# Giving the two operations that split a half block of weights a place ahead of all others in the scheduler

## The chip, the cores and the metric

The kernel runs on one core of one Trainium2 chip. The metric is the device time of one execution in microseconds (us); lower is better. Engines are called PE (TensorE, matrix products; PEld is its weight loading), DVE (VectorE), ACT (ScalarE), POOL (GpSimd) and SP (SyncE, which issues the DMAs). Each takes its instructions in one fixed order.

## The reference

Two residual blocks follow each other on x, 512 positions by 2048 channels, float32. What is computed, cut to the steps that cost time:

```
# first block
h = rms_norm(x) * (1 + scale) + shift;  p = h @ w_in
u = layer_norm(conv31(cv * sigmoid(cg)));  y_conv = (silu(u) * silu(cz)) @ w_conv_out
y_attn = (rms_norm(differential attention, 8 heads) * silu(az)) @ w_attn_out
x = x + gate * rms_norm((sigmoid(m1) * y_conv + sigmoid(m2) * y_attn) @ w_o)
# second block, on x (512 positions, "lat") and a context (256 positions, "ctx")
u = h @ w_in2                                  # h: 512 x 2048, w_in2: 2048 x 8,608
gated delta rule, 8 heads, both directions:    # conv5, l2norm, then by chunks of 64
    T = inverse(I + L);  v_new = T v - T k state;  o = q state + attn v_new
    state = state * decay + k^T v_new
RWKV-7 scan, 16 heads, both directions, by chunks in the kernel
x = rms_norm(x + gate * concat(delta rule, RWKV) @ w_out)
```

## The kernel before

A product with a weight matrix is called dense here. `mblock` makes 128 output columns in one accumulator (`pd`, two buffers) out of 16 blocks of 128 rows, in two half blocks of eight. `products` does a half block: one DMA brings 512 KB into `wraw` (three buffers), the split makes two reduced float32 parts of it, `whi` (a cast on ACT, line 105) and `wlo` (the difference, on DVE, line 106; during the first products of the context every second one is on POOL), each with two buffers, and 24 matmuls of line 157 follow: whi with the high part of the activations, whi with their low part, wlo with the high part, eight times. A half block can be cast when its `wraw` has landed and the matmuls of the half block before the last have let go of its `whi`.

The order on each engine is made by a list scheduler ahead of the run: among the instructions that its own model of time finds ready it takes the one with the lowest priority number, and the number grows with the order in which the program is written. `tc.cur_priority -= FIRST` (a million) puts what is issued until it is set back ahead of all else. In `products` that holds for the matmuls except every twelfth (`K.burst`; every sixth in the later parts), so that dense matmuls come in groups that nothing interrupts and between groups PE can turn to something else. In the same way `before` in the RWKV part adds 800 (`LATER`) to everything that the dense products written there issue.

The parts of the run that are spoken of: the products of the context with the delta rule's inputs (about 420 to 640 us of the trace), the delta rule on x (`mixers_gdn`, 2240 to 2950 us) and the RWKV part on x (`mixers_rwkv`, to 3830 us). In the delta rule each of eight heads is a sequence of three stretches, and the dense blocks of the next head (q, k, v, z, two half blocks each) are worked in between:

- preparation: Gram products (line 632), masks on DVE (`gd_kkd` and others), the first part of a triangular inverse on DVE (`iv_u8`, `iv_sh`, lines 368 to 383);
- the inverse on PE (lines 396 to 432, 692 to 717), with copies on ACT and DVE between;
- the chain over four steps (line 123 in `Visit.mm`): a product with `gd_uu` gives on DVE `gd_vn` (line 755), a product with `gd_ktl` gives the state `S` (line 775), a product with `S` gives `gd_R` (line 747), and so on. Each step waits for the one before.

The RWKV part has a similar chain: the products into `pc` and, on DVE, `rg_H` (lines 1060 and 1077).

Of the kernel before, what the change touches and what calls it, by code (L numbers as in the profile page):

```python
# [103 lines left out]
def split(K, hi, lo, src, eng=None):  # L104
    K.nc.scalar.copy(hi, src)  # L105
    (eng or K.nc.vector).tensor_tensor(lo, src, hi.bitcast(F32), op=ALU.subtract)  # L106


FIRST = 1000000
# [22 lines left out]
def mblock(K, wap, act, T, k0=0, k1=16, half=8):  # L132

    ps = K.pd.tile([128, 512], F32, name="pd")
    for ka in range(k0, k1, half):
        products(K, ps, wap, act[ka - k0:], T, ka, min(half, k1 - ka), k0, k1)
        K.fill()
    return ps[:, :T]


def products(K, ps, wap, act, T, ka, w, k0, k1):


    nc, tc = K.nc, K.tc
    raw = K.wp.tile([128, 8, 128], F32, name="wraw")
    hi = K.wp.tile([128, 8, 128], F32R, name="whi", bufs=2)
    lo = K.wp.tile([128, 8, 128], F32R, name="wlo", bufs=2)
    nc.sync.dma_start(raw[:, :w], wap[:, ka:ka + w, :])
    K.n_split += 1
    split(K, hi[:, :w], lo[:, :w], raw[:, :w], nc.gpsimd if K.on_pool and K.n_split % K.on_pool == 0 else nc.vector)  # L150
    for k in range(w):
        ah, al = act[k]
        for j, (a, b) in enumerate(((hi, ah), (hi, al), (lo, ah))):
            n = 3 * (ka - k0 + k) + j
            ahead = FIRST if n % K.burst else 0
            tc.cur_priority -= ahead
            nc.tensor.matmul(ps[:, :T], lhsT=a[:, k], rhs=b, start=(n == 0), stop=(n == 3 * (k1 - k0) - 1))  # L157
            tc.cur_priority += ahead
# [199 lines left out]
def inv64(K, pool, upool, nm, ds, px, tmp):  # L358
# [30 lines left out]
    for lev in range(2):  # L389
        yp, zp = products()  # L390
        ys = pool.tile([128, n, 32], F32, name="iv_y")
        for m in range(n):
            for r in range(4):
                q = slice(32 * r, 32 * r + 32)
                o = 32 * (r % 2)
                nc.tensor.matmul(yp[q, m], lhsT=nm[q, m, o:o + 32], rhs=t32[q, m], start=True, stop=True,
                                 tile_position=(32 * r, 32 * r))
        nc.scalar.copy(ys, yp)
        for m in range(n):
            for r in range(4):  # L400
                q = slice(32 * r, 32 * r + 32)
                nc.tensor.matmul(zp[q, m], lhsT=ys[q, m], rhs=u32[q, m], start=True, stop=True,  # L402
                                 tile_position=(32 * r, 32 * r))
        for d, m0, w in orders:
            nc.vector.copy_predicated(u32[:, m0:m0 + w], K.cp[d, lev].unsqueeze(1).to_broadcast([128, w, 32]),  # L405
                                      zp[:, m0:m0 + w])
        nc.vector.transpose(t32.rearrange("p n e -> p (n e)"), u32.rearrange("p n e -> p (n e)"))

    u64 = upool.tile([128, n, 64], F32, name="iv_u64")
    for b in range(2):  # L410
        nc.vector.tensor_scalar(u64[:, :, 32 * b:32 * b + 32], u32, c["m64"][:, b:b + 1], None, op0=ALU.mult)
    yp, zp = products()
    ys = pool.tile([128, n, 32], F32, name="iv_y")

# [1432 lines left out]
```

## Time and profile before

| | |
|---|---|
| three runs | 3966.07, 3958.37, 3956.31 us (median 3958.37) |
| the profiled execution | 3948.75 us, of which the span from first to last instruction is 3947.0 us |
| PE busy | 3672.7 us, 93% of the span |
| DVE / ACT / POOL busy | 70% / 34% / 13% |
| mean granted clock of PE | 0.962 of full speed |

A busy share counts the time in which an instruction of the engine is under way; matmuls overlap, so one may last 0.4 us while they follow each other every 0.23 us. In a view of waits the numbers are the total wait in us, the number of times and the longest. In a timeline a row gives the start, the time until the end of the group, engine, line, operation, output<-input and count, and in brackets how long the engine sat idle before it and what ended that. In a table of windows each engine has its busy us and number of instructions; the three numbers at the end are PE's granted clock (1.00 is 2.4 GHz, 0.50 is 1.2 GHz), the busy share of the DMA engines, and GB/s.

### The profile page before, as it was taken

The page shows a single profiled execution, that of the slowest core. Times are in us where ns is not written, and L with a number is a line of the kernel's source. Part 1 is how long each engine was busy: PE and PEld are TensorE (multiplying, and loading weights), DVE is VectorE, ACT ScalarE, POOL GpSimd, SP SyncE. Part 2 cuts the span into 40 slices and gives each one's busy share as a digit, 9 for nine tenths or more (in the row PEclk, how much of TensorE's full clock was granted, in tenths as well). Part 3 has the DMA queues.
Part 4 walks back from the last instruction along what each step waited for, and adds up shares of the span by engine and source line. Part 5 has one row for each costly group of instructions (what it writes and reads, how often), then busy time and mean ns, then how long its engine had stood idle before and what let it go on. Part 6 is the DMA issues. An engine that isn't in the chain of part 4 may idle for free. (4 is left out here: it accounts for less than half of the span.)

```text
span 3947.0 us, 81802 instructions
## 1 busy us (share of the span) xinstructions
PE 3672.7 (93%) x33066; PEld 2837.3 (72%) x33066; DVE 2748.4 (70%) x7146; ACT 1359.4 (34%) x2713; POOL 505.4 (13%) x595
## 2 busy tenths in 40 slices
PE   8899878999999999999998889989999999998997
PEld 4577678876777777777886577777877777766676
DVE  3366798788778778553524877776767778877866
ACT  3322333323334344332322432322323444444333
POOL 0100231003101001000311201100001111111102
PEclk9999899999999999999999999999999999999998
DMA  8766445423433333425523222222223122212235
GB/s 321 269 226 216 161 133 173 140 102 127 136 118 107 118 111 126 130 81 179 204 93 129 101 88 68 67 69 75 86 79 110 65 68 81 68 67 83 91 129 203
DMA packets 206491, 492.95 MB, mean 125 GB/s; under 512 B 40096, under 2 KB 71328, under 8 KB 202016
## 3 DMA queue, kind: packets, MB, share of 16 engines
q1 hardware_dynamic: 206112, 487.72, 36.4%
q8 instruction: 260, 4.26, 0.4%
q14 instruction: 119, 0.97, 0.1%
HBM read 434.54 MB, written 53.09 MB: 124 GB/s over the span
## 5 line engine op out<-in xcount | busy, mean ns | idle before, releaser
L157 PE MATMUL pd<-big,whi 128*128 128x512 f32 x5280 | 1759.5, 411 | 8.0 <-ACT big L352 8.0
L157 PEld LDWEIGHTS pd<-big,whi 128*128 128x128 f32 x5280 | 964.4, 192 | 251.4 <-issue 20.8
L157 PE MATMUL pd<-big,wlo 128*128 128x512 f32 x2768 | 1104.2, 399 | 24.3 <-DVE wlo L106 23.6
L105 ACT CAST whi<-wraw 128x1024 fp32r<-128x1024 f32 (+2 forms) x498 | 502.9, 1010 | 1159.5 <-PE pd L157 1074.7
L106 DVE TENSOR_TENSOR wlo<-wraw,whi 128x1024 fp32r<-128x1024 f32 (+2 forms) x478 | 572.9, 1199 | 318.4 <-ACT whi L105 311.2
L157 PEld LDWEIGHTS pd<-big,wlo 128*128 128x128 f32 x2768 | 530.0, 191 | 147.1 <-DVE wlo L106 28.2
L157 PE MATMUL pd<-hc,whi 128*128 128x256 f32 x1152 | 227.0, 297 | 11.5 <-ACT hc L352 5.5
L157 PE MATMUL pd<-hc,wlo 128*128 128x256 f32 x576 | 171.7, 298 | 33.0 <-DVE wlo L106 23.9
L157 PEld LDWEIGHTS pd<-hc,whi 128*128 128x128 f32 x1152 | 188.3, 199 | 15.3 <-ACT hc L352 5.6
L157 PE MATMUL pd<-ext,whi 128*128 128x512 f32 x512 | 184.6, 401 | 3.8 <-DVE ext L106 3.8
L1160 DVE SCALAR_TENSOR_TENSOR cv_y<-cv_up,vec,cv_y 128x512 f32<-128x512 f32 x240 | 180.9, 754 | 4.2
L157 PE MATMUL pd<-fa,whi 128*128 128x512 f32 x448 | 149.9, 414 | 0.9 <-ACT fa L105 0.8
L157 PEld LDWEIGHTS pd<-hc,wlo 128*128 128x128 f32 x576 | 114.8, 199 | 40.0 <-DVE wlo L106 28.0
L944 POOL TENSOR_TENSOR rg_bk<-rg_th,rg_L 64x512 f32<-64x512 f32 x48 | 69.1, 1439 | 400.5 <-ACT rg_L L923 274.0
L1055 ACT ACTIVATE rg_zw<-rg_H,rg_wc 64x64 f32<-64x64 f32 x320 | 102.8, 342 | 43.4 <-DVE rg_H L1077 39.2
L157 PEld LDWEIGHTS pd<-ext,whi 128*128 128x128 f32 x512 | 97.3, 190 | 27.9 <-DVE ext L106 4.7
L1077 DVE SCALAR_TENSOR_TENSOR rg_H<-pc,rg_wc,rg_zw 64x64 f32<-64x64 f32 x320 | 90.4, 282 | 33.7 <-PE pc L123 24.0
L567 DVE SCALAR_TENSOR_TENSOR gc_y<-gc_up,vec,gc_y 128x512 f32<-128x512 f32 (+1 forms) x160 | 108.6, 679 | 2.8 <-issue 0.2
L242 DVE SCALAR_TENSOR_TENSOR ada_ev<-wraw,cs_ada,ada_ev 128x512 f32<-128x512 f32 x120 | 93.7, 781 | 20.3 <-DMA wraw<-in_wada_dram 18.9
L157 PEld LDWEIGHTS pd<-fa,whi 128*128 128x128 f32 x448 | 80.7, 190 | 21.8 <-ACT fa L105 1.9
L157 PE MATMUL pd<-fa,wlo 128*128 128x512 f32 x224 | 89.1, 398 | 0.7 <-DVE wlo L106 0.7
L405 DVE COPY_PREDICATED iv_u<-cpi,px 128x256 f32<-128x256 int32 (+2 forms) x112 | 35.2, 340 | 73.2 <-PE px L402 62.8
(589 smaller groups left out, 5592.9 us busy)
## 6 DMA issues: line engine op xcount, KB each, us to landing
wraw<-in_w_dram SPq DMA_DIRECT2D x366, 512.0 KB, 3.6
wraw<-in_wada_dram SPq DMA_DIRECT2D x128, 512.0 KB, 4.5
wraw<-in_wada_dram SPq DMA_DIRECT2D x32, 1024.0 KB, 4.8
wraw<-in_wo_dram SPq DMA_DIRECT2D x32, 512.0 KB, 3.5
sgl<-sgd SPq DMA_DIRECT2D x48, 256.0 KB, 3.3
wraw<-in_wout_dram SPq DMA_DIRECT2D x20, 512.0 KB, 3.8
wraw<-in_w_dram SPq DMA_DIRECT2D x36, 256.0 KB, 3.6
sgd<-msg SPq DMA_DIRECT2D x32, 256.0 KB, 3.3
```

The lines of the kernel that those rows point to most:

```text
L105: K.nc.scalar.copy(hi, src)
L106: (eng or K.nc.vector).tensor_tensor(lo, src, hi.bitcast(F32), op=ALU.subtract)
L157: nc.tensor.matmul(ps[:, :T], lhsT=a[:, k], rhs=b, start=(n == 0), stop=(n == 3 * (k1 - k0) - 1))
L242: nc.vector.scalar_tensor_tensor(ev, raw[:, k], cs[:, kk, 0:1], ev, op0=ALU.mult, op1=ALU.add)
L405: nc.vector.copy_predicated(u32[:, m0:m0 + w], K.cp[d, lev].unsqueeze(1).to_broadcast([128, w, 32]), zp[:, m0:m0 + w])
L567: nc.vector.scalar_tensor_tensor(y, up[:, t:t + T], w[:, t:t + 1], y, op0=ALU.mult, op1=ALU.add)
L944: nc.gpsimd.tensor_tensor(bk[uq, :, u], th[uq], F[uq], op=mul)
L1055: nc.scalar.activation(zw[hv[u], d], H[hv[u], ms[d], u], AF.Copy, scale=wn[hv[u], 4 * d + mn])
L1077: nc.vector.scalar_tensor_tensor(Hn[hv[u], 4 * d + mn, u], pc3[hv[u], 2, d], wn[hv[u], 4 * d + mn], zw[hv[u], d], op0=mul, op1=ALU.add)
L1160: nc.vector.scalar_tensor_tensor(y, up[:, t:t + 512], w[:, t:t + 1], y, op0=ALU.mult, op1=ALU.add)
```

## The change

The lines of the split are enclosed in the same change of priority that the matmuls have; nothing is added or taken away.

```diff
     nc.sync.dma_start(raw[:, :w], wap[:, ka:ka + w, :])
     K.n_split += 1
+
+    tc.cur_priority -= FIRST
     split(K, hi[:, :w], lo[:, :w], raw[:, :w], nc.gpsimd if K.on_pool and K.n_split % K.on_pool == 0 else nc.vector)
+    tc.cur_priority += FIRST
     for k in range(w):
```

The number of instructions stays the same on each engine, and so do the two orders of the half blocks among themselves. What moves is how the splits stand against the rest, and with them, since the scheduler goes on from there, the dense matmuls against the rest. In the rows below line numbers after the change are three higher from line 153 on. The number behind a name tells one tile from another of that name.

On DVE, in the delta rule at the change from the fifth head's preparation to its inverse, before (`wlo_24743` is the first half of v of the next head; `gd_kkd` stands 23 rows further up):

```order
L207 SCALAR_TENSOR_TENSOR gq_24601<-gc_th_24602,gc_y_24595 128x512
L1132 SCALAR_TENSOR_TENSOR gz_23081<-gz_23081,po_23655 128x512
L370 TENSOR_REDUCE iv_n8_24102<-iv_tmp_24099 128x32
L1133 SCALAR_TENSOR_TENSOR gz_23081<-gd_o_23213,vec_80,gz_23081 128x512
L375 TENSOR_TENSOR iv_u8_24104<-iv_u8_24104,iv_n8_24102 128x4
L368 TENSOR_TENSOR iv_tmp_24099<-gd_dd_24014,cst_78 128x256
L377 STREAM_SHUFFLE iv_sh_24106<-iv_u8_24104 128x32
L565 TENSOR_SCALAR gc_y_24700<-gc_up_24696,vec_80 128x512
L378 TENSOR_TENSOR iv_sh_24106<-iv_sh_24106,iv_n8_24102 128x32
L106 TENSOR_TENSOR wlo_24743<-wraw_24741,whi_24742 128x1024
```

and with the change:

```order
L210 SCALAR_TENSOR_TENSOR gz_23948<-gc_th_24010,pd_23949 128x512
L178 SCALAR_TENSOR_TENSOR go_rs_y_23639<-go_rs_t_23640,go_rs_y_23639 128x4
L750 SCALAR_TENSOR_TENSOR gd_R00_24396<-pc_24393,TM_lat_21019,gd_vt_24025 128x128
L750 SCALAR_TENSOR_TENSOR gd_R10_24398<-pc_24393,TM_lat_21019,gd_vt_24025 128x128
L570 SCALAR_TENSOR_TENSOR gc_y_24595<-gc_up_24591,vec_80,gc_y_24595 128x512 x2
L106 TENSOR_TENSOR wlo_24743<-wraw_24741,whi_24742 128x1024
L1135 SCALAR_TENSOR_TENSOR gz_23081<-gz_23081,po_23655 128x512
L641 TENSOR_TENSOR gd_kkd_24055<-px0_24038,cst_78 128x256
L1136 SCALAR_TENSOR_TENSOR gz_23081<-gd_o_23213,vec_80,gz_23081 128x512
L669 TENSOR_TENSOR gd_at_24086<-gd_dd_24014,gd_qkd_24076 64x8x64
```

The split has moved from behind the head's masks and the start of its inverse to a place ahead of `gd_kkd`; five heads have this pattern.

On PE, in the chain of the same head, steps two to four, before (`whi_24637` and `wlo_24638` are the first half of k of the next head):

```order
L123 MATMUL po_23599<-gd_at_23219,gd_vn10_23594 128x128
L123 MATMUL po_23599<-gd_egt_23146,S_10_23578 128x128
L123 MATMUL po_23599<-gd_at_23219,gd_vn00_23592 128x128
L123 MATMUL po_23599<-gd_egt_23146,S_00_23576 128x128
L157 MATMUL pd_24635<-big_20483,whi_24637 128x512
L157 MATMUL pd_24635<-big_20484,whi_24637 128x512
L157 MATMUL pd_24635<-big_20483,wlo_24638 128x512
L157 MATMUL pd_24635<-big_20489,whi_24637 128x512
L157 MATMUL pd_24635<-big_20490,whi_24637 128x512
L157 MATMUL pd_24635<-big_20489,wlo_24638 128x512
L123 MATMUL pc_23610<-S_10_23606,gk_22972 128x128
L123 MATMUL pc_23610<-S_00_23604,gk_22972 128x128
```

and with the change:

```order
L123 MATMUL pc_23596<-gd_vn10_23594,gd_ktl_23523 128x128
L123 MATMUL pc_23596<-gd_vn00_23592,gd_ktl_23523 128x128
L123 MATMUL po_23599<-gd_at_23219,gd_vn10_23594 128x128
L123 MATMUL po_23599<-gd_egt_23146,S_10_23578 128x128
L123 MATMUL po_23599<-gd_at_23219,gd_vn00_23592 128x128
L123 MATMUL po_23599<-gd_egt_23146,S_00_23576 128x128
L123 MATMUL pc_23610<-S_10_23606,gk_22972 128x128
L123 MATMUL pc_23610<-S_00_23604,gk_22972 128x128
L123 MATMUL pc_23617<-gd_R10_23615,gd_uu_23497 128x128
L123 MATMUL pc_23617<-gd_R00_23613,gd_uu_23497 128x128
L160 MATMUL pd_24635<-big_20483,whi_24637 128x512
L160 MATMUL pd_24635<-big_20484,whi_24637 128x512
```

The groups of six dense matmuls that stood between the steps of the chain are gone from there; they stand before and behind it. Four heads have this pattern.

On DVE, in the RWKV part, around one step of the chain before:

```order
L1060 TENSOR_SCALAR rg_H_30812<-pc_31158 64x2x64
L546 TENSOR_TENSOR rg_L_32111<-rg_L_32111 128x128
L546 TENSOR_TENSOR rg_L_32111<-rg_L_32111 128x64
L995 TENSOR_TENSOR rg_nr_31362<-px0_31377,cst_78 64x512
L1077 SCALAR_TENSOR_TENSOR rg_H_30812<-pc_31158,rg_wc_30783,rg_zw_31171 64x64 x4
```

and with the change:

```order
L1063 TENSOR_SCALAR rg_H_30812<-pc_31158 64x2x64
L549 TENSOR_TENSOR rg_L_32111<-rg_L_32111 128x64
L549 TENSOR_TENSOR rg_L_32111<-rg_L_32111 128x32
L106 TENSOR_TENSOR wlo_31773<-wraw_31771,whi_31772 128x1024
L1080 SCALAR_TENSOR_TENSOR rg_H_30812<-pc_31158,rg_wc_30783,rg_zw_31171 64x64 x4
```

A split now stands directly ahead of the step. In this part 24 of 72 splits do on DVE, 16 before.

## Rows read from the trace of the kernel before

**Rows 1.** The page: span, and busy us of PE, PEld, DVE, ACT, POOL.

```profile
span 3947.0 us, 81802 instructions
PE 3672.7 (93%) x33066; PEld 2837.3 (72%) x33066; DVE 2748.4 (70%) x7146; ACT 1359.4 (34%) x2713; POOL 505.4 (13%) x595
```

**Rows 2.** Waits of PE in the whole span (us, times, longest).

```profile
PE pd L157 <- DVE wlo L106: 48.1, 24, 4.5
...
PE pd L157 <- POOL wlo L106: 8.8, 14, 2.0
```

**Rows 3.** Waits of PE from 2400 to 2950 us.

```profile
PE pd L157 <- DVE wlo L106: 22.6, 5, 4.5
```

**Rows 4.** Waits of PE from 400 to 700 us.

```profile
PE pd L157 <- DVE wlo L106: 23.9, 16, 4.3
```

**Rows 5.** Timeline of PE in the fifth head of the delta rule.

```profile
2573.96 0.79 PE L157 MATMUL pd<-big,wlo 128*128 128x512 f32 x1 [4.51 <-DVE wlo L106]
...
2577.11 1.05 PE L157 MATMUL pd<-big,whi 128*128 128x512 f32 x2
...
2582.04 0.61 PE L157 MATMUL pd<-big,whi 128*128 128x512 f32 x2
...
2587.48 0.61 PE L157 MATMUL pd<-big,whi 128*128 128x512 f32 x2
...
2588.66 0.74 PE L396 MATMUL px<-iv_t,gd_dd 32*32 32x32 f32 x64 [0.34 <-issue]
```

**Rows 6.** Timeline of DVE, same head.

```profile
2558.42 0.16 DVE L168 TENSOR_SCALAR go_rs_xh<-po 128x4 f32<-128x4 f32 x1 [0.96 <-PE po L837]
...
2563.79 0.41 DVE L638 TENSOR_TENSOR gd_kkd<-px,cst 128x256 f32<-128x256 f32 x1
...
2572.69 1.22 DVE L106 TENSOR_TENSOR wlo<-wraw,whi 128x1024 fp32r<-128x1024 f32 x1
...
2588.12 0.45 DVE L383 STREAM_TRANSPOSE iv_t<-iv_u 128x256 f32<-128x256 f32 x1
```

**Rows 7.** Timeline of ACT, same head.

```profile
2567.51 1.04 ACT L105 CAST whi<-wraw 128x1024 fp32r<-128x1024 f32 x1 [0.90 <-PE pd L157]
```

**Rows 8.** Windows of one head's period: chain, preparation, inverse.

```profile
2530.56:2557.44 26.88, 25.66 (x162) 22.46 (x161) 19.79 (x58) 7.02 (x15) 4.33 (x8) 1.00 0.17 58
2557.44:2588.66 31.22, 26.37 (x172) 21.02 (x171) 29.09 (x106) 9.96 (x16) 2.34 (x6) 0.89 0.20 68
2588.66:2609.77 21.11, 21.11 (x429) 15.86 (x430) 9.91 (x22) 6.11 (x12) 1.57 (x6) 1.00 0.28 84
```

**Rows 9.** Timeline of PE in the chain of that head.

```profile
2537.94 0.61 PE L123 MATMUL pc<-gd_R,gd_uu 128*128 128x128 f32 x4
...
2545.42 0.61 PE L123 MATMUL pc<-gd_R,gd_uu 128*128 128x128 f32 x4
2547.20 0.71 PE L123 MATMUL pc<-gd_vn,gd_ktl 128*128 128x128 f32 x4 [1.18 <-DVE gd_vn L755]
...
2551.94 0.61 PE L123 MATMUL pc<-gd_R,gd_uu 128*128 128x128 f32 x4
```

**Rows 10.** Timeline of DVE in the same chain.

```profile
2538.59 0.61 DVE L755 TENSOR_SCALAR gd_vn<-pc,TM_lat 128x128 f32<-128x128 f32 x2 [1.32 <-PE pc L123]
```

**Rows 11.** Windows in the products of the context.

```profile
466.00:620.00 154.00, 122.07 (x888) 114.72 (x888) 137.22 (x271) 54.16 (x86) 51.71 (x52) 0.94 0.41 137
552.00:568.00 16.00, 12.79 (x98) 11.92 (x98) 13.97 (x24) 5.76 (x9) 5.86 (x6) 1.00 0.44 152
```

**Rows 12.** Windows in the RWKV part.

```profile
3114.00:3131.00 17.00, 13.61 (x140) 10.13 (x138) 14.52 (x55) 5.60 (x10) 5.45 (x4) 0.92 0.26 87
3131.00:3138.00 7.00, 7.00 (x149) 5.67 (x150) 5.25 (x9) 2.76 (x4) 0.00 (x0) 0.70 0.24 83
```

**Rows 13.** Waits of DVE from 2950 to 3640 us.

```profile
DVE wlo L106 <- ACT whi L105: 15.1, 10, 3.4
```

## The prediction

> **What bounds the kernel now.** I began with the page's first part [rows 1]: PE is busy 3672.7 of 3947.0 us, the next engine, DVE, 2748.4. PE carries the time, and the change adds no work to it; what can be won is a share of PE's 274 us without an instruction, and of the time in which its clock is low.
>
> Next the waits of PE, since the change moves the two instructions that a dense matmul waits for. The wait for `wlo` made on DVE is 48.1 us in 24 times, up to 4.5 us each, and for `wlo` made on POOL 8.8 us in 14 times [rows 2]. By stretches: 22.6 us are five waits of about 4.5 in the delta rule on x [rows 3], 23.9 us are sixteen in the products of the context [rows 4]. Waits for `whi` are too small to carry a term. So 57 us is all that a split in time could save directly.
>
> Then one of the five places, on three engines. PE's timeline [rows 5] shows it idle for 4.51 us until 2573.96. After that two matmuls take 1.05 us (2577.11) where they take 0.61 later: half clock, from 2573.96 to past the pair at 2577.11, some 4.2 us, which at full speed would be 2.1. At full rate 24 matmuls lie between 2582.04 and 2587.48, so one is 5.44/24 = 0.227 us. DVE's timeline [rows 6] shows the split at 2572.69 for 1.22 us, after a queue of the delta rule's work. ACT's [rows 7] shows that its cast was done long before (2567.51 + 1.04 = 2568.55), after a wait of 0.90 for PE to release the buffer. So the split is late because of its place in DVE's queue, and the new order changes that place.
>
> Last, the windows of this head's period [rows 8]: chain 26.88, preparation 31.22, inverse 21.11, together 79.2 us. In the preparation DVE is busy 29.09 of the 31.22. And at its end PE takes the inverse's first product at 2588.66 [rows 5] just after DVE ended the transpose that it reads, 2588.12 + 0.45 = 2588.57 [rows 6]. So in this stretch the 4.5 us that PE waits are not what sets its end: DVE is. That decides how I read the change.
>
> **Preparation: what a split in time is worth there.** With the change the split stands ahead of `gd_kkd`, and some work that DVE does now at the stretch's start (from `go_rs_xh` at 2558.42 to `gd_kkd` at 2563.79, 5.4 us [rows 6]) stands ahead of the stretch, under the chain. DVE after: cast 1.0 to 1.2 after the buffer is free [rows 7], the split 1.2, and what runs now from 2563.79 to 2588.57, 24.8 (one split leaves it, another comes in), less some 0.4 for smaller work ahead: 26.8. PE after: by the order 102 dense matmuls stand in this stretch instead of 78, since the four sixes between the chain's steps come here. They cost 102 × 0.227 = 23.2. The rest of PE's work is now 31.22 − 4.51 − 2.1 − 78 × 0.227 = 6.9; of this some 2.1 (the products on k, v and S at the stretch's start) stand ahead of it after the change, and fewer turns from one kind of product to another take about 0.5 less, an estimate: 4.3. Together 27.5, a little over DVE's 26.8. So 31.2 becomes 27.5, a gain of 3.7 in each of five heads, 18.5 us. Bounds: nothing, if DVE's early work isn't hidden under the chain; 4.5 + 2.1 = 6.6 each, 33 us, if wait and half clock vanish and nothing comes back.
>
> **Inverse.** Same rows on each engine in both orders, 60 dense matmuls in both: 0.
>
> **Chain: what is given back.** Here the dense matmuls leave. Now the chain takes 21.4 us from the first product with `gd_uu` (2530.56 [rows 8]) to the fourth (2551.94 [rows 9]) and 5.5 to the stretch's end. A bare hop costs 0.65 us from the product at 2537.94 to DVE's start at 2538.59 [rows 9, 10], then DVE's 0.61 and a little: 1.3. With another group queued on PE in between it is 1.78 (2545.42 to 2547.20 [rows 9]). Six dense matmuls cost 6 × 0.227 = 1.36, so each covers a hop almost exactly; PE idles 1.2 us of 26.88 [rows 8]. After the change, by the order: to the fourth product with `gd_uu` 2.65 for the first step as now, eight hops of 1.3 (10.4), 1.7 for a split that stands directly between two halves of the state on DVE (1.22 and its turn), and 2.0 for other groups queued: 16.75. Behind it 11.7 for what stood between the steps and still belongs to the stretch (four sixes, 5.4, the norm's products, those on k and v): together 28.4, 1.5 more than now. Bounds by the same rows: all hops at 1.3 and the split hidden 23.5, every hop at 1.78 and more 30.1, so −3.4 to +3.2. Four heads have the pattern: 4 × 1.5 = 6.
>
> **The clock.** In this bare stretch PE would idle about 6.4 of 17 us. What that does shows in two places: in the context 12.79 busy of 16 us stay at a granted clock of 1.00 [rows 11]; in the RWKV part 13.61 busy of 17 us are followed by 7 us at 0.70 [rows 12]. A mean of 0.70 is 60% at half speed, 4.2 us that would take 2.1. So 0 to some 2.4 per bare chain; our case is idler than either, and I take half, 1.2, since the idle is cut into pieces of about 1 us and not one of 4.5: 4 × 1.2 = 5. The delta rule together: −18.5 + 6 + 5 = −7.5.
>
> **Context.** Its 23.9 us of waits look like the same prize, but DVE is busy 137.22 of 154 us [rows 11], and only part of the splits move, by two to seven rows. What PE wins in one place it waits for in another, because DVE's sum is unchanged. The largest waits that end earlier come to about 10, the bound; nothing is the other; I take −2.
>
> **RWKV.** Here 24 splits of 72 instead of 16 stand directly ahead of a step of the chain on DVE. Each costs 1.22 there: 8 × 1.22 = 9.8, or 8 × (1.22 + 1.04) = 18 if DVE also waits for the cast. That it can is seen now: DVE waits 15.1 us in ten times for casts [rows 13]. Behind it are the chain's next products on PE, and dense matmuls hide about half: +5, between 0 and 18.
>
> **Everything else** (casts on ACT: 332 of 498 don't move; splits on POOL; SP's queue): 0. ACT is busy a third of the time, and a cast that moves ahead by a row or two delays work of about 1 us that isn't on the path.
>
> **The sum.** −7.5 − 2 + 5 = −4.5 us on the profiled execution: 3948.75 becomes 3944. That execution lies 9.6 us under the median of the runs, so the median goes to about 3953.5, −0.1%. With all good bounds: −33 − 14 − 10 = −57; with all bad ones: 0 + 4 × (3.2 + 2.4) + 0 + 18 = +40.
>
> **Rivals.** (1) Faster. The chain stays hidden: PE's queue lets the dense groups run ahead or the hops overlap so that the 24 moved matmuls fit without loss. Then the five waits and their half clock go: 33 us, −2 and +5 for the rest: 3928. For it: the preparation gets all its matmuls at 0.227 and PE is the fullest engine. Against it: DVE ends the preparation, not PE [rows 5, 6], and the hops are bare in the order.
>
> (2) Slower, by the clock in the bare chains. If PE falls to half speed there, eight hops grow by about 0.45 each (0.61 for a group becoming 1.05) and the next 30 dense matmuls by 0.2: 3.6 + 6 = 9.6 for a chain. Then −18.5 + 4 × (1.5 + 9.6) − 2 + 5 = +29: 3987. It decides when the clock is at half for some 7 us more in each head than now (4 × 7 × 0.5 = 14 against the gain). For it: rows 12, and that a single wait of 4.51 us brings half clock [rows 5]. Against it: 12.79 of 16 at 1.00 [rows 11]. A rule speaks for this rival: the Trainium skill, TensorE: Matmul & The Clock Gate, section "A second HAM failure mode: psum-queue depth-cycling", tells of a kernel whose PE idled briefly but often between groups, so that the clock swung between its two levels and throughput suffered from it. The rows of this kernel agree in the RWKV part and not in the context.
>
> (3) Slower, in the RWKV part. By the order the dense matmuls there fall up to 72 behind the chain about the fourth pair of heads, and make it up later. If it isn't made up under the chain, 72 × 0.227 = 16 us are exposed, with the 9.8 in full: −9.5 + 26 = +16: 3975. It decides if dense work runs bare at the part's end. Against it: at the part's end both orders stand level.
>
> (4) Nothing moves: waits end elsewhere and the time stays at 3958.
>
> **How the numbers follow.** What a measurement here can tell from no change is about 0.3%, 12 us. The forecast (waits go, most is given back) has 0.38, rival 4 0.05, both within 0.3%: 0.43. Rival 1 has 0.33: faster. Rival 2 has 0.15 and rival 3 0.09: slower 0.24. Range: down to 3924, since rival 1 may win a little more than its 33 with the context's −10; up to 3979, which takes in rival 3 and the lower part of rival 2. Some 0.05 lie below and 0.12 above.
>
> **What the profile would show.** Right: the five waits of 4.5 for `wlo` are gone, the preparation is 27 to 28 us instead of 31.2 and its clock near 1.00; the chain's window is 28 to 29, with PE busy for under 21 and waits for `gd_vn`, `gd_R` and `S` in the list of waits; the inverse stays at 21.1; the context's waits for `wlo` keep more than half of their sum. A chain of 27 or less with the preparation at 27 is rival 1; a clock below 0.8 in the chain, and a preparation that is still 30 or more, is rival 2. The prediction goes wrong most easily by the hops: 0.3 us on each of eight in four heads is 10 us.

## The result, and the profile after

The change makes the kernel slower: 4006.94 us median of four runs where the kernel before had 3957.34 beside it, a ratio of 1.012 with a 95% interval of 1.009 to 1.015. In a second batch of runs (after_again below) it was 1.0079, from 1.0061 to 1.0097. The forecast was −0.1%, and its range ended half a per cent above the kernel before.

The page of the changed kernel, span and busy us, which answers to [rows 1]:

```profile
span 4009.3 us, 81820 instructions
...
PE 3738.3 (93%) x33066; PEld 2884.7 (72%) x33066; DVE 2748.2 (69%) x7146; ACT 1361.3 (34%) x2713; POOL 513.9 (13%) x595
```

This is the reading that decides the case. The span grew by 62.3 us, and PE's busy time by 65.6. PE without an instruction: 4009.3 − 3738.3 = 271 us, before 274. So nothing that the change did to waits is left in the total; PE does the same 33,066 matmuls and needs longer for them. The mean granted clock says why: 0.962 before, 0.948 now. At two levels, 2.4 and 1.2 GHz, that is 2 × 0.038 × 3947 = 300 us at half speed before and 2 × 0.052 × 4009 = 417 now, 117 us more, of which half, 58, is lost. Not all of that is time in which PE works; summed from the trace's records of the clock and of PE's instructions, over the three stretches below, PE was busy at half clock for 161 us before and for 297 after. Half of the difference, 68 us, is about what its busy time grew by.

The waits did go where the change aimed. Waits of PE in the whole span, to be read beside [rows 2]:

```profile
PE px L399 <- issue: 23.6, 12, 8.2
PE pd L160 <- DVE wlo L106: 20.5, 16, 5.6
...
PE pd L160 <- POOL wlo L106: 6.8, 12, 1.1
```

and in the context, beside [rows 4]:

```profile
PE pd L160 <- DVE wlo L106: 19.5, 14, 5.6
```

The five long waits of the delta rule on x are gone; the context keeps four fifths of its own. In their place stands the inverse's first product (L399), which waits for what DVE makes; the same line of the kernel before:

```profile
PE px L396 <- issue: 8.2, 11, 1.5
```

Three times the sum, and the longest 8.2 us instead of 1.5.

Where the time went is read from three stretches, cut in both kernels at the same dense matmuls: the rest of the first block, the delta rule on x, the RWKV part on x. Before, and after (windows as in [rows 8]):

```profile
723.66:2079.74 1356.08, 1315.50 (x10549) 1008.21 (x10548) 907.75 (x2413) 464.67 (x956) 151.52 (x154) 0.98 0.38 126
2079.74:2959.56 879.82, 802.67 (x6957) 638.62 (x6955) 621.13 (x1674) 266.90 (x447) 105.29 (x184) 0.96 0.25 84
2959.56:3890.60 931.04, 874.31 (x11289) 659.33 (x11288) 710.32 (x2026) 379.14 (x905) 116.40 (x96) 0.95 0.28 94
```

```profile
722.92:2095.86 1372.94, 1325.30 (x10557) 1014.86 (x10556) 921.88 (x2434) 464.17 (x957) 161.11 (x156) 0.98 0.37 124
2095.86:2985.48 889.62, 814.14 (x6956) 650.05 (x6955) 621.88 (x1674) 267.36 (x447) 107.35 (x184) 0.95 0.25 83
2985.48:3953.30 967.82, 918.09 (x11289) 692.46 (x11287) 703.29 (x2026) 381.42 (x905) 114.96 (x96) 0.90 0.28 90
```

The first block lost 16.9 us, the delta rule 9.8, the RWKV part 36.8. In the RWKV part PE idled 967.8 − 918.1 = 49.7 us, 7 less than before (56.7), while its clock fell from 0.95 to 0.90. By the same records, PE's busy time at half clock rose from 35.1 to 52.0 us in the first block, from 42.5 to 60.0 in the delta rule and from 83.1 to 185.2 in the RWKV part; half of each rise is 8.5, 8.8 and 51 us. In the delta rule that is nearly all of the loss, since PE idles 1.7 us less there.

One caution on these differences: the profiled execution of before was a quick one, 9.6 us under the median of its runs, so single profiles put the losses somewhat too high.

The delta rule, one head's period, as in [rows 8]:

```profile
2551.21:2583.36 32.15, 27.60 (x158) 23.62 (x156) 22.07 (x73) 8.51 (x18) 4.92 (x9) 0.84 0.14 42
2583.36:2612.00 28.64, 27.08 (x176) 22.31 (x175) 27.25 (x92) 8.58 (x13) 2.15 (x6) 1.00 0.23 83
2612.00:2633.11 21.11, 21.11 (x428) 15.72 (x429) 9.73 (x21) 6.11 (x12) 1.57 (x6) 1.00 0.22 70
```

Preparation 31.22 to 28.64 and at full clock, inverse unchanged to the hundredth, chain 26.88 to 32.15 at a clock of 0.84. PE's timeline inside that chain shows the fall, with the waits behind it:

```profile
2561.23 0.68 PE L123 MATMUL pc<-S,gk 128*128 128x128 f32 x4
2563.12 1.05 PE L840 MATMUL px<-cst,gc_th 128*128 128x1 f32 x8 [1.22 <-ACT gc_th L575]
2564.39 1.22 PE L123 MATMUL pc<-gd_R,gd_uu 128*128 128x128 f32 x4 [0.21 <-DVE gd_R L750]
2566.31 1.22 PE L123 MATMUL pc<-gd_vn,gd_ktl 128*128 128x128 f32 x4 [0.70 <-DVE gd_vn L758]
...
2570.80 1.22 PE L123 MATMUL pc<-gd_R,gd_uu 128*128 128x128 f32 x4 [0.70 <-DVE gd_R L750]
```

The same group of four took 0.61 to 0.71 before; here it takes 1.22.

The RWKV part falls in another way. Two windows of the changed kernel:

```profile
3092.00:3104.00 12.00, 9.30 (x245) 7.20 (x236) 11.68 (x25) 5.33 (x18) 6.19 (x6) 0.99 0.20 69
3104.00:3131.00 27.00, 27.00 (x203) 20.05 (x202) 12.57 (x39) 11.46 (x31) 0.00 (x0) 0.50 0.07 24
```

For 27 us some matmul is under way on PE at every moment, and the clock is at half; in the 12 us before it PE was busy for 9.30, with a pause of 2.27 us until 3101.99. What runs in the 27 us is the chain, the products around it (32x32 to 96x256) and 19 dense matmuls in groups of six, which take 11.5 us. In the kernel before, 60 us of this part at a clock of 1.00 (3062 to 3122) hold 108 dense matmuls.

### The profile page after: what moved, and what is told of

It is laid out like the page before. It is cut to its first block, busy times and chain, and to the rows that moved or that the text cites. A ratio compares the mean times of both kernels' runs of the same rounds, so it can differ in the third digit from the quotient of the medians.

```text
span 4009.3 us, 81820 instructions
## 1 busy us (share of the span) xinstructions
PE 3738.3 (93%) x33066; PEld 2884.7 (72%) x33066; DVE 2748.2 (69%) x7146; ACT 1361.3 (34%) x2713; POOL 513.9 (13%) x595
## 5 line engine op out<-in xcount | busy, mean ns | idle before, releaser
L160 PE MATMUL pd<-big,whi 128*128 128x512 f32 x5280 | 1769.9, 413 | 11.5 <-ACT big L355 8.1
L160 PE MATMUL pd<-hc,wlo 128*128 128x256 f32 x576 | 170.1, 296 | 26.7 <-DVE wlo L106 19.5
L995 PE MATMUL px<-rg_C,rg_bk 64*128 64x128 f32 x512 | 94.5, 324 | 2.6 <-DVE rg_C L998 2.6
```

The source lines that it names most:

```text
L995: nc.tensor.matmul(pg[:, m], lhsT=bk[q, 4 * r + m].rearrange("p x c -> p (x c)"), rhs=C[q, 4 * r + m, u], start=True, stop=True, tile_posi ...
```

## The experiments

I began with three theories for the loss. Theory 1: in the new order the dense matmuls are thinned out along the chains, and what PE does there instead, short waits and small products, costs it the clock. Theory 2: splits that stand directly ahead of a chain's step on DVE delay it. Theory 3: the loss is spread over all places where a split moved. All ratios below are against the kernel before, measured beside the run; a stretch's length is from the one profiled execution. Comments in the code cuts are notes for the reader.

**One part of the run at a time.** The priority became a number that is set for each part; the order on PE then is that of the change in that part, and that of before elsewhere.

```diff
-    tc.cur_priority -= FIRST
+    tc.cur_priority -= K.ahead
     split(K, ...)
-    tc.cur_priority += FIRST
+    tc.cur_priority += K.ahead
...
-        K.burst = 6
+        K.burst, K.ahead = 6, 0        # gdn_only: FIRST
         mixers_gdn(K, blk)
-        K.burst = 6
+        K.burst, K.ahead = 6, FIRST    # rwkv_only; 0 in the other two
...
-    K.burst = 12
+    K.burst, K.ahead = 12, 0           # first_only: FIRST
```

rwkv_only: 

> The split goes ahead of all others only in the RWKV part on x; all else is ordered as before. Theory 1 (thinned dense work: the dense matmuls fall up to 84 behind the chain, PE is busy with small products and sits at half clock for about 188 us of this part instead of 89): most of the loss is here, +30 to +40 us, and PE idles no more in this part than before. Theory 2 (splits that stand directly ahead of a chain step on DVE, 36 with the change and 25 before): the loss is here too, but PE's idle time in the part grows. Theory 3 (the loss is spread over the run, a little wherever a split moved): +15 or less.

gdn_only: 

> The split goes ahead only in the delta rule on x. The trace of the changed kernel lost 10 us there. My prediction's terms for this part alone gave -7.5 us. Theory 1, with the bare chains paying in clock: +5 to +12. Theory 2: +2 to +5 (11 splits ahead of a step, 8 before). Theory 3: about +10.

first_only: 

> The split goes ahead only in what precedes the second block's mixers on x (first block, all of the context). The trace of the changed kernel was 15 us late at the end of that stretch, 5 of them before anything in it had moved much. Theory 1 (only where dense work is thinned): +5 to +12. Theory 2 (splits ahead of chain steps): 0 to +5, since there is hardly a chain. Theory 3: +15 or more.

rwkv_only had 1.0021 (1.0000 to 1.0042), gdn_only 1.0015 (0.9998 to 1.0032), first_only 1.0017 (0.9998 to 1.0037). Each part costs 0.15 to 0.2%, the delta rule among them, though two of the three intervals reach to just below 1; none alone is what I expected of the RWKV part. That went for theory 3, until the stretches were read. The delta rule's is 889.75 us in gdn_only and 879.82 in rwkv_only: it repeats what the two first profiles had to about a tenth. The first block's is 1375.9 in first_only. The RWKV stretch does not repeat so well: with the order of before it was 931.0 (before), 934.8 (gdn_only) and 945.9 (first_only), and over all seven profiles with that order 931.0 to 946.1, on average 937; with the order of the change it was 967.8 and, in rwkv_only:

```profile
2964.16:3910.73 946.57, 896.23 (x11289) 676.98 (x11287) 703.59 (x2026) 381.69 (x905) 113.81 (x96) 0.93 0.29 92
```

Again less idle than before (946.6 − 896.2 = 50.3) and a lower clock. So part of the 62 us between the two first profiles was the lot of a single execution, and 946.6 alone, at the upper end of the range for the order of before, shows no loss.

**The whole once more, and without the RWKV part.**

after_again: 

> The whole change once more, on the chip of the runs above, because the three parts alone measured +0.21%, +0.15% and +0.17%, together 0.53%, where the whole had 1.2%. If the parts add up (each costs what its own order costs), +0.5%, about 3988 us where before is 3967; if the parts make each other worse, +1% or more. The delta rule's stretch is again 10 us longer and the first block's 17 us; the RWKV stretch lies anywhere between the +15.5 and the +36.8 us of the two profiles of its order.

no_rwkv: 

> The split goes ahead of all others everywhere except in the RWKV part on x. If the parts add up: the sum of the two alone, +0.32%, about +13 us. If the RWKV part is what makes the whole expensive, +0.3% or less here, and the difference to the whole change is 0.7% or more.

after_again had 1.0079 (1.0061 to 1.0097), no_rwkv 1.0048 (1.0030 to 1.0066). The RWKV part is worth 0.31% in company and 0.21% alone: the parts add up within their intervals. after_again's stretches were 1373.8, 888.5 and 945.2 us, 17.7, 8.7 and 14.2 over the profile of before. Both totals lie above my range; which of 0.8 and 1.2% is typical I can't say; the two intervals share 0.90 to 0.97%.

**One operation of the two.**

```diff
-    tc.cur_priority -= FIRST
-    split(K, hi[:, :w], lo[:, :w], raw[:, :w], ...)
-    tc.cur_priority += FIRST
+    nc.scalar.copy(hi[:, :w], raw[:, :w])
+    tc.cur_priority -= FIRST            # sub_only; in cast_only the two lines
+    (...).tensor_tensor(lo[:, :w], ...) # stand around the copy
+    tc.cur_priority += FIRST
```

sub_only: 

> Only the subtraction goes ahead of all others, the cast stays where it was, in the whole run. In the order 34 subtractions then stand directly ahead of a step of the RWKV chain (36 with both, 25 before), but the dense matmuls are on the average 5 ahead of where they stood before instead of 19 behind. Theory 1: the RWKV part loses little or gains, the whole within -10 to +15 us of before, half clock in the part near 89 us. Theory 2: the RWKV part loses as with both, the whole +30 to +50. Theory 3: half of the loss, about +25.

cast_only: 

> Only the cast goes ahead of all others, the subtraction stays where it was, in the whole run. By the order the delta rule's chains keep their dense matmuls (18, 12 and 12 between the steps); in the RWKV part the dense matmuls stand on the average 7 behind where they stood before (19 behind with both, 5 ahead with the subtraction alone), with 27 subtractions directly ahead of a step (25 before, 36 with both). Theory 1 (clock, from thinned dense work): delta rule's stretch unchanged within 2 us, the RWKV stretch +3 to +12 with more half clock than before. Theory 2 (splits ahead of a step): the RWKV stretch unchanged. In the first block the subtraction alone cost 17 us, so here 0 to 5.

rwkv_sub (subtraction alone, RWKV part alone): 

> Only the subtraction, and only in the RWKV part on x, goes ahead of all others. The RWKV stretch was 3 us shorter in the profile of sub_only. Theory 1: -5 to +4 us for the whole, no measurable loss, against +0.21% for both operations there. Theory 2: as rwkv_only, +8 or more.

sub_only had 1.0009 (0.9994 to 1.0023), cast_only 1.0013 (0.9994 to 1.0032), rwkv_sub 0.9975 (0.9956 to 0.9994). The RWKV stretch in the three, in this order:

```profile
2991.13:3919.10 927.97, 878.39 (x11288) 663.68 (x11287) 701.98 (x2026) 382.48 (x905) 115.58 (x96) 0.95 0.29 94
```

```profile
2969.29:3915.98 946.69, 896.56 (x11288) 676.79 (x11287) 701.56 (x2026) 381.17 (x905) 112.07 (x96) 0.93 0.28 93
```

```profile
2973.28:3900.97 927.69, 881.15 (x11289) 665.27 (x11287) 701.83 (x2026) 382.35 (x905) 115.64 (x96) 0.94 0.29 94
```

Theory 2 falls here, by rwkv_sub, which has more subtractions ahead of a step and is faster, beyond the best that I had expected (−5 us). The numbers of subtractions ahead of a step in the expectations (25, 36, 34 and 27) count the context's RWKV run too; in the part on x alone they are 16 before, 24 with both operations, 22 with the subtraction and 21 with the cast. So the last two are alike in this. With the subtraction ahead the stretch is 928.0 and 927.7 us (923.8 in a third profile, fill_gdn_cheap_rwkv_sub below), less than in any of the seven profiles with the order of before. With the cast it is 946.7 at a lower clock, just above the seven; by the stretch alone that is no more than a sign, and the clocks of all executions decide it below. In the other stretches it is the subtraction that costs: sub_only has 1373.4 and 890.1 us there, as the change, and cast_only has 880.3 in the delta rule, though its first block is 9.0 us longer than in the profile of before, where I had put 0 to 5. In these single profiles the two losses of sub_only come to 28 us, while its whole measured 0.09%; most of that gap is the quick profile of before, 3948.75 us, where the median in this batch is 3966.95. rwkv_sub is a version that beats the kernel before, by a quarter of a per cent (0.06 to 0.44).

**Making the lag without the split.** The cast alone also makes the dense matmuls fall behind the RWKV chain in the order, the subtraction alone doesn't. That could be the cause, or a bystander of the casts' place on ACT.

```diff
-AHEAD, LATER = 2, 800
+AHEAD, LATER = 2, 1000
```

before_later1000: 

> The kernel before, no split moved in rank, but LATER 1000 instead of 800 in the RWKV part. By the order the dense matmuls there then stand behind the chain as they do with the change (first to last pair, by half pairs: 6, 6, 0, -54, -54, -60, -66, -36, -42, 12, 0, 0, -4, 0, -6, 6; with the change 0, -24, -18, -54, -54, -48, -72, -30, -42, 12, 12, 12, 32, -6, -12, 18). Theory 1 (dense work that falls behind the chain costs the clock): the RWKV stretch is 8 to 20 us longer with 30 us or more of additional half clock, the whole +0.2 to +0.4%. Theory 4 (it is the casts' own place on ACT, ahead of the chain's copies, that costs; the lag is a bystander): the stretch within 5 us of before, the whole within 0.1%.

The ratio is 1.0054 (1.0030 to 1.0078). The RWKV stretch:

```profile
2957.54:3919.42 961.88, 905.48 (x11288) 683.07 (x11287) 711.10 (x2026) 381.33 (x905) 112.74 (x96) 0.92 0.28 91
```

30.8 us longer than in the profile of before, more than the 8 to 20 expected, with the same idle time (961.9 − 905.5 = 56.4) and a clock of 0.92. No split was given a higher rank; the kernel differs from the one before in one number that sets all of the dense work back, its casts and subtractions with the matmuls. By the trace 21 subtractions stand directly ahead of a step in it, where before has 16 and rwkv_sub, which is faster, 22. Theory 1 holds in this part, and theory 4 of that expectation isn't needed.

**The clock of every execution.** The mean granted clock of each run is on record, not only that of the profiled one. (1 − clock) × span is then what an execution lost to half clock, if PE had work all the time. Averages over the runs, each against the kernel before beside it:

| | clock, and that of before | lost to half clock, more by | time, more by |
|---|---|---|---|
| after_again | 0.9498, 0.9600 | 42 us | 33 us |
| before_later1000 | 0.9550, 0.9608 | 24 us | 21 us |
| rwkv_only | 0.9538, 0.9581 | 17 us | 9 us |
| cast_only | 0.9570, 0.9601 | 13 us | 8 us |
| sub_only | 0.9577, 0.9581 | 2 us | 6 us |
| rwkv_sub | 0.9603, 0.9601 | −1 us | −10 us |

The standard errors of these differences are 2 to 4.5 us. Wherever the order lets the dense matmuls fall behind the RWKV chain, the clock falls, and that accounts for all of the added time; with the subtraction alone it stays. What remains when the clock's share is taken off is 8 us less than before both in rwkv_only and in rwkv_sub. So subtractions ahead of the chain save time in this part, and with the cast ahead as well the clock takes more than they save.

**Covering the idle time of the bare chains.** In the delta rule theory 1 says that half clock eats the gain. Products that nothing reads were put behind the groups of the chain in the four heads where it is bare. They change the order too: dense matmuls come back between the steps.

```diff
+        def cover(vis, p, n):
+            if lat and hs[0] in (1, 2, 3, 4):
+                for _ in range(n):
+                    vis.mm(p[:, 256:512], lhsT=c["ident"], rhs=vt[:, 0, 0:2]..., start=True, stop=True)
...
                 vis.mm(reg(p, d, j), lhsT=ks[j][:, tts[d]], rhs=S[j][d], start=True, stop=True)
+            cover(vis, p, 2)
...
             vis.mm(reg(p, d, j), lhsT=uu[:, d, j, ts[d]], rhs=R[d, j], start=True, stop=True)
+        cover(vis, p, 2)
```

fill_gdn_202: 

> As gdn_only (split ahead in the delta rule on x only), with idle PE time covered: in the four heads whose chain is bare, two extra products of 128x256, whose output nothing reads, follow the products with gd_uu and those with the state, 14 in a head. By the order dense matmuls come back between the steps too (18, 0, 12 instead of 6, 0, 0). Theory 1 (bare chains cost most by half clock): the half-clock time of 10.2 us per chain falls to 3.4 or less and the delta rule's stretch is 10 to 25 us shorter than in gdn_only. Rival (the hops themselves cost, the clock follows by accident): the stretch is as long as in gdn_only or longer by the extra products, 14 x 0.22 = 3 us for each of four heads.

fill_gdn_313: 

> As fill_gdn_202 with three, one and three extra products, 24 in a head; by the order 12, 12 and 12 dense matmuls stand between the four steps of these chains. Theory 1: half clock in the chains is gone (3.4 us or less each), the stretch is 5 to 20 us shorter than in gdn_only though PE has 4 x 24 x 0.22 = 21 us more work. Rival: longer than gdn_only by 10 to 20 us.

fill_gdn_202 had 1.0032 (1.0015 to 1.0048), fill_gdn_313 1.0077 (1.0054 to 1.0100). Windows over five heads, of gdn_only and of fill_gdn_202:

```profile
2400.00:2800.00 400.00, 374.29 (x3781) 304.42 (x3780) 291.68 (x899) 115.00 (x209) 40.89 (x94) 0.95 0.22 69
```

```profile
2400.00:2800.00 400.00, 379.59 (x3889) 308.05 (x3888) 291.47 (x905) 114.14 (x207) 40.44 (x98) 1.00 0.22 69
```

The clock is back to 1.00 in all five heads, though PE still idles 20.4 us of 400. But the stretch is 890.1 us, as long as in gdn_only, and this half of the expectation missed. One row says why:

```profile
2566.39 1.03 PE L123 MATMUL pc<-gd_vt,cst 128*128 128x256 f32 x4
```

The two products are four rows: each takes two passes, about 0.43 us, not the 0.22 that I had put in. So 14 in a head cost 6 us and four heads 24. Over the whole stretch PE idles 67.3 us instead of the 75.3 of gdn_only, 8 less, so the clock must have given back some 16; the trace's records agree, with 26.7 us busy at half clock instead of 58.8, of which half is 16. With 24 products in a head the stretch is 911.5 us, 22 longer than in gdn_only, and that expectation missed too. These runs show that the clock can be held, and that this way of holding it costs what it brings. How much of it the extra products do, and how much the dense matmuls that come back with them, they don't separate.

**A cheaper cover, and the best parts together.**

```diff
-                    vis.mm(p[:, 256:512], lhsT=c["ident"], rhs=vt[:, 0, 0:2]..., start=True, stop=True)
+                    vis.mm(p[:, 256:512], lhsT=c["ident"].bitcast(bfloat16)[:, 0:128],
+                           rhs=c["ident"].bitcast(bfloat16)[:, 0:256], start=True, stop=True)
```

fill_gdn_cheap: 

> As fill_gdn_202, but the extra products are in bfloat16 and so take one pass of 256 columns instead of two: 14 in a head, an estimate of 0.11 us each (half of the 0.215 of one pass in fill_gdn_202's trace), 1.5 us for each of four heads instead of 6. By the order 12, 6 and 12 dense matmuls stand between the steps. Theory 1: the chains keep full clock, and the delta rule's stretch is 10.3 - 4 x 4.5 = -8 us against before, -4 to -12. Rival: as gdn_only, +10.

fill_gdn_cheap_rwkv_sub: 

> fill_gdn_cheap in the delta rule and rwkv_sub in the RWKV part together, nothing ahead in the first block: if both do what they should, -8 - 3 = -11 us, -0.3%; a version that beats both kernels. If the clock in the chains is not what cost there, +5 or more.

fill_gdn_cheap had 1.0022 (1.0001 to 1.0044), both together 1.0003 (0.9985 to 1.0022). Both expectations missed. The five heads in fill_gdn_cheap:

```profile
2400.00:2800.00 400.00, 376.60 (x3872) 307.05 (x3872) 295.61 (x907) 115.64 (x210) 42.78 (x97) 0.97 0.21 69
```

The short cover doesn't hold the clock (0.97), and the stretch is 885.8 us, 6 above before. Together with rwkv_sub its loss takes that one's gain.

## Why the prediction was wrong, point by point

What failed in common is the price of half clock. The prediction booked 2.1 us less of it in each of five preparations and 5 us more in the chains, −5.5 us in all, and none in the RWKV part and the first block; after_again lost 42 us more to it than the kernel before.

**The waits and the preparation: right.** The five waits went. DVE sets the end of the preparation, as read from [rows 5, 6]: the transpose ends on DVE at 2611.90, PE takes the product at 2612.00. The two rows, DVE and PE:

```profile
2611.45 0.45 DVE L386 STREAM_TRANSPOSE iv_t<-iv_u 128x256 f32<-128x256 f32 x1
```

```profile
2612.00 0.74 PE L399 MATMUL px<-iv_t,gd_dd 32*32 32x32 f32 x64 [1.56 <-issue]
```

28.64 us against 27.5: splits take 5.00 us of DVE in five pieces where the kernel before has 3.77 in four (some cut by the window's ends), and I had let one in for the one that leaves. The inverse, 0: right.

**The chain: the mechanism right, the clock's term too small.** I put the bare chain at 28.4 us and took 1.2 for the clock, "since the idle is cut into pieces". The window has 32.15 us at a clock of 0.84, so 0.32 × 32.15 = 10.3 us at half speed, worth up to 5.1. Without that it would be some 27 to 28: the hops were sized well. Half clock moved from the preparations (6.8 us of each, by 0.89 in [rows 8]) into the chains, where I had booked its end as a gain. Per head the forecast was −3.7 + 1.5 + 1.2 = −1.0, and 81.90 − 79.21 = +2.7 was measured; the whole stretch +8.7 to +10.3 in five profiles, −7.5 forecast. Over the stretch PE's busy time at half clock grew by 17.5 us: before, 36 of its 78.5 us at half clock passed while PE stood idle, and now 29 of 88.7 do. Rival 2 was the case here: 11.1 for chain and clock together where 5.3 was measured on the chain's window, its direction and cause right. The rule that I weighed beside it (the Trainium skill, TensorE: Matmul & The Clock Gate, section "A second HAM failure mode: psum-queue depth-cycling") agrees with this trace: pauses of 0.2 to 1.2 us between groups, and 0.84.

**The RWKV part: the step that failed.** "Each costs 1.22 there: 8 × 1.22 = 9.8 [...] dense matmuls hide about half: +5." Splits ahead of the chain cost nothing that can be seen: rwkv_sub, with 22 of them, is 10 us faster. What costs is what rival 3 named, the dense matmuls that fall behind, and at a price that I had put at nothing: not exposed PE time, since PE idles 6.4 to 11.5 us less in the three profiles with the order of the change, but its clock, from 0.95 to between 0.90 and 0.93. before_later1000 makes the lag without moving a split in rank; its stretch is +30.8 us in the profile, its whole time +21 with 24 more lost to half clock. By the runs the part is worth 0.21% alone and 0.31% in company, 8 to 12 us. That lies within my bounds of 0 to 18 by luck, since what they were made of did not happen. How much a given lag costs stays open: the cast alone has a third of the mean lag of both and the same stretch (946.7 and 946.6).

**The first block: a term that I put at 0.** "Everything else [...]: 0." The stretch is 16.9 to 19.8 us longer in all profiles with the subtraction ahead (five), between 3 shorter and 9 longer in those without. The largest piece is one wait. DVE, in the first block, after:

```profile
920.33 0.65 DVE L384 TENSOR_SCALAR iv_u<-iv_u,cst 128x16 f32<-128x16 f32 x4
920.89 1.22 DVE L106 TENSOR_TENSOR wlo<-wraw,whi 128x1024 fp32r<-128x1024 f32 x1
922.03 0.31 DVE L386 STREAM_TRANSPOSE iv_t<-iv_u 128x128 f32<-128x128 f32 x1
```

PE there, after, and the same product before:

```profile
922.43 0.65 PE L399 MATMUL px<-iv_t,gd_dd 32*32 32x32 f32 x32 [8.16 <-issue]
```

```profile
915.20 0.45 PE L396 MATMUL px<-iv_t,gd_dd 32*32 32x32 f32 x32 [1.45 <-issue]
```

A split now stands directly ahead of the transpose that PE waits for, and the inverse's serial steps on DVE come later as a whole: 8.16 us of idle PE instead of 1.45, and half clock after it (1.22 us for the next pair of dense matmuls, by the timeline). I had looked at which splits move far, and here they move by few rows; what moved is the inverse's steps behind them. The split itself is 1.22 us of this. Most of the rest comes from POOL, which was at work when the later steps ran. After, a step beside a POOL operation, and the same step without one:

```profile
918.38 1.26 POOL L1177 TENSOR_TENSOR cn_t<-cn_t,cn_mean 128x512 f32<-128x512 f32 x1
918.48 1.18 DVE L382 TENSOR_TENSOR iv_u<-iv_u,iv_sh 128x16 f32<-128x16 f32 x1
920.12 0.18 DVE L382 TENSOR_TENSOR iv_u<-iv_u,iv_sh 128x16 f32<-128x16 f32 x1
```

The step ends when POOL's operation does. Nine steps of this inverse take 0.94 to 1.33 us in that way instead of less than 0.2, and three did before; that is some 5.7 us more, and all five profiles with the subtraction ahead show it. The wait is also nearly all of the stretch's additional idle time: 6.0 to 8.0 us in these five, −1.8 to +2.2 in the others. What is left of the loss is busy time, most of it at half clock (35.1 us before, 52.0 after). With the order of before it is 30.3 to 52.9, so how much of that part the change makes stays open.

**The context:** −2 forecast. Its waits kept more than half of their sum, as I had said. The dense matmul at which the next stretch is cut starts at 722.92 against 723.66, but in the other profiles it starts anywhere between 723.18 and 730.87, whichever the order. So the term does no harm, and 2 us can't be seen here.

**The chances.** The two slower cases had 0.24, priced one at a time. The first came in the delta rule. Of the second the condition came, dense work that falls behind, but not its price: what was exposed was not the dense work but half clock, the first one's cause. That the case was slower was thus in the chances, its size was not: no rival had the clock in the RWKV part, or the first block.

## What to carry to other kernels

When PE is over 90% busy, read its busy time and its granted clock before its waits: a reordering can take away the waits that it aims at and lose by what PE does in between. Ask of a list scheduler's change not only where the favoured instruction goes, but which long matmuls it pulls out of the stretches that need them as cover; the order shows that before a run, as the count of dense matmuls between a chain's steps. And try the two operations of such a pair apart, part by part of the program: here the subtraction alone in one part gained 0.25% where both everywhere lost 0.8 to 1.2%. Where a single profile varies by more than the term, the clock that is recorded with every run settles what one stretch can't.

## What the runs showed of the hardware that was not expected

PE at 27.00 us busy of 27.00 ran at half clock (0.50) where its work was products of 32x32 to 96x256 with 19 dense ones between; I had thought of idle time alone as what lowers the clock. Busy means here that a matmul is under way, not that the array is full, and a pause of 2.27 us stood shortly ahead. The Trainium skill (TensorE: Matmul & The Clock Gate, section "Part 1: The HAM clock gate (the "warmup" mystery)") says that the gate follows how busy PE has been; in this trace a PE that the profile calls fully busy did not get its clock. Conversely, with 20 us idle in 400 it kept 1.00 when the pauses of the chain were filled with 256-column products in float32, and not (0.97) with the shorter ones in bfloat16. By the orders 30 dense matmuls of a head stand between the steps with either.

A small DVE operation beside a POOL operation can last until that one ends: 1.18 us instead of 0.18 for a step of the inverse in the first block, and nine such steps in one inverse of the changed kernel.

One execution's share of half clock is not fixed by the order: the same RWKV order had 931.0 to 946.1 us in seven profiles, and in one batch of 35 runs of the kernel before the quickest took 3942.79 us at a clock of 0.965 and the longest 3983.26 at 0.955. So a single profile can't size a term of 10 us in that part; the delta rule's stretch, 879.8 to 881.3 in five, can.
